# Fifteen instead of fourteen pairs of gate tiles by seven products, with three differences of h released from the pinned order

## The chip, the cores and the metric

The kernel runs on one core of a Trainium2 chip. The metric is the device time of one execution in microseconds (us), lower is better. TensorE (PE) multiplies, VectorE (DVE) and ScalarE (ACT) work elementwise, GpSimd (POOL) does some elementwise work and issues DMAs that add into their target, SyncE (SP) issues the other DMAs. Each engine takes its instructions in the order in which they stand in its own list, and waits on semaphores for the others.

## The reference, cut to what matters

Two groups of tokens go through one layer: 128 context tokens and 512 tokens of a grid, 640 together. Of the layer only the middle matters here:

```
h = rmsnorm(x, norm1_g) * (1 + sc1) + sh1            # 1024 features, 640 tokens
proj = h @ w_in                                      # input of four mixers a, b, c, d
y_a = gated short convolution; y_b = HGRN2 (a scan); y_c = neighbourhood attention; y_d = gMLP
g_a, g_b, g_c, g_d = split(sigmoid(h @ w_gate + b_gate), 4)
merged = g_a * (y_a @ w_br_a) + g_b * (y_b @ w_br_b) + g_c * (y_c @ w_br_c) + g_d * (y_d @ w_br_d)
x = x + g1 * (merged @ w_o)                          # then norm2 and the ConvFFN
```

`w_gate` is 1024 by 4096, each `w_br` 256 by 1024. A gate tile is 128 of the 1024 output features of one mixer, for all 640 tokens.

## The kernel before, in words

Features lie on the 128 partitions, tokens along a row. Every float32 operand is split into a high and a low part of type float32r, and every product is three matmuls (high by high, high by low, low by high), each 128x128 by 320 tokens. The high part is a copy by ScalarE, the low part a difference by VectorE.

**Plain gate tile** (`gate_tile`, line 997): 8 slices of features of h, and 2 of the mixer's y, in two halves of the tokens, three matmuls each: (8 + 2) x 2 x 3 = 60 matmuls by `gemm` (line 375 is the matmul). Its low part is made with a DMA by POOL (`low_dma`).

**Pair by seven products** (`g_pair`, line 1236): tiles n and n+4 of a mixer are computed together. Features are cut into two halves and tokens into two halves, so weights and h are 2 by 2 blocks, and seven products of sums of blocks (the scheme of Strassen and Winograd) replace eight. Each product is 12 matmuls over h (`gprod`, line 1186) and 3 over y (`bprod`, line 1195): 7 x 15 = 105 for the pair. In each pair the products over h stand in the order 1, 2, 6, 5, 7, 4, 3, with those over y between them. The sums of weight blocks for pair n+1 are made by VectorE while TensorE works on pair n (`g_s01`, `g_s23`, `g_b`, `g_c`, `g_zh`). `PAIRS` (line 990) lists them; `NPL` (line 46) says how many of the four pairs of the first mixer, d, are left to plain tiles. With `NPL = 2` four tiles of d (0, 1, 4, 5) are plain, and 14 pairs follow.

**Operands of the pairs** (`g_operands`, line 1038, a generator that is stepped beside the tiles): the products 7, 5 and 6 need sums of blocks of h. The float32 h waits in device memory (`hdr`, four blocks by feature half and token half). Three blocks are loaded: `d[:, 0]` and `d[:, 1]` (tile D) and `g` (tile G). Line 1051 makes three differences in place: a22 = a21 - a22, a21 = a11 - a21, a11 = a22 - a11, each 128x1280 on VectorE. `g_split` (lines 1077 and 1078) splits them into the tiles F (product 7), X1 (product 5) and X0 (product 6); F is free after the attention's last scores (`"scores"`), X1 and X0 after its last output (`"yc"`). Then the fourth block is loaded over a22 (line 1064), `y_load` (line 1080) puts y_d into D with a load by SP and an accumulating load by POOL, line 1071 adds a22 and a11, and `y_sums` (line 1089) makes four differences of y in D, from which `y_split` fills tile C.

**Order.** A helper keeps a clock of TensorE work and steps the side jobs (attention, convolution, operands) at due times on it, so program text is emitted interleaved. A scheduler of the framework may then move an instruction within its engine's list, unless `tc.keep_in_program_order` pins it. The differences of line 1051 are pinned; the whole pair part is pinned too (`fixed`, `ovec`, `oact`). `g_all` (line 1339) first drains the side jobs until the operands are emitted.

**Around the change** TensorE runs the attention's steps (scores at lines 842 and 845, transposes at 862, outputs at 879) between the last tiles of w_in and the first plain gate tiles. VectorE adds the bias and takes the maximum (849, 851), scales the exponentials (858, 859) and copies transposes back (2272).

Of the kernel before, what the change touches and what calls it, by code (L numbers as in the profile page):

```python
# [13 lines left out]
ALU = mybir.AluOpType  # L14
# [28 lines left out]
""".split()  # L43
WARM = 100
UE = [5, 3, 1]
NPL = 2
LOWD = ("ac", "ax", "ab", "d")
T = 640
TS = 512
# [21 lines left out]
def tile_step(ctx: ExitStack, tc: tile.TileContext, a: dict, outs: list, dbg=None):  # L71
# [58 lines left out]
    def region(tag, shape, dt=F32):  # L130
        return big.tile(shape, dt, tag=tag, name=nm(tag))
# [23 lines left out]
    ten, vec, pool = [Ordered(e, boot) for e in (nc.tensor, nc.vector, nc.gpsimd)]  # L155
# [236 lines left out]
    R = {}  # L392
# [524 lines left out]
    def in_tile(sec, n, w):  # L917
        ps = pg()
        gemm(ps, w, 0, 8, xhk, xlk)
        evac_in(sec, n, ps)  # L920
        if n == 1:
            R[sec + "_done"] = True
        if n == 1 and sec in starts:
            start(starts[sec](), 1.5, SLACK[sec])
            if sec == "cv":
                start(g_operands())
        if (sec, n) == AE[0]:
            start(ada_cols(range(16, AE[3]), "S0", col_home, HD[4], 10), AE[1])
# [60 lines left out]
    GI = dict(a=0, b=1, c=2, d=3)  # L989
    PAIRS = [(0, n) for n in range(NPL, 4)] + [(bi, n) for bi in range(1, 4) for n in range(4)]  # L990
    GPAIR = len(PAIRS)
# [46 lines left out]
    def g_operands():  # L1038
        while "cg" not in R:
            yield 1  # L1040
        d, g = region("D", [P, 2, 4, HC]), region("G", [P, 4, HC])
        yield 8
        for x, h, c in ((d[:, 0], 0, 1), (d[:, 1], 1, 1), (g, 0, 0)):
            yield 10
            nc.sync.dma_start(x, hdr[h, c])
        while "ya" not in R:
            yield 1
        yield 5
        a21, a22, a11 = d[:, 0], d[:, 1], g
        for o, x, y in ((a22, a21, a22), (a21, a11, a21), (a11, a22, a11)):  # L1050
            tc.keep_in_program_order(vec.tensor_tensor(o, x, y, ALU.subtract))
            yield 2
        gx["x"] = {}
        for i, h, c in ((1, 0, 0), (2, 1, 0), (4, 1, 1), (3, 0, 1)):
            cs = slice(c * HC, (c + 1) * HC)
            gx["x"][i] = xh[:, 4 * h:4 * h + 4, cs], xl[h][:, :, cs]
        for i, x, t, key in ((7, a21, "F", "scores"), (5, a22, "X1", "yc"), (6, a11, "X0", "yc")):
            while key not in R:
                yield 1
            y = region(t, [P, 2, 4, HC], F32R)  # L1060
            gx["x"][i] = y[:, 0], y[:, 1]
            g_split(i, x)
            if i == 5:
                nc.sync.dma_start(a22, hdr[1, 0])
            yield 1.5
        gx["t3"] = a22, a11
        gx["Y"] = a21.rearrange("p a t -> p (a t)")
        gx["S"] = a22.rearrange("p a t -> p (a t)").rearrange("p (i k c) -> p i k c", i=2, k=5)
        y_load(0)
        yield 7  # L1070
        vec.tensor_tensor(a22, a22, a11, ALU.add)
        y_sums()
        R["gx3"] = True

    def g_split(i, x):
        h, l = gx["x"][i]
        act(h, x, AF.Copy)
        vec.tensor_tensor(l, x, h.bitcast(F32), ALU.subtract)

    def y_load(bi):  # L1080

        if bi < 2:
            h, l = [R["y" + BR[bi]][:, i].rearrange("p k t -> p (k t)").bitcast(F32) for i in range(2)]
        else:
            h, l = [(ybd if bi == 2 else ycd)[:, i].rearrange("p k t -> p (k t)") for i in range(2)]
        nc.sync.dma_start(gx["Y"], h)
        opool.dma_start(gx["Y"], l, accum_op=ALU.add)

    def y_sums():

        a11, a21, a12, a22 = [gx["Y"][:, i * HC:(i + 1) * HC] for i in range(4)]
        for o, x, y, f in ((a22, a21, a22, ALU.subtract), (a21, a11, a21, ALU.subtract),
                           (a11, a22, a11, ALU.subtract), (a12, a12, a11, ALU.add)):
            ovec.tensor_tensor(o, x, y, f)
# [18 lines left out]
    def gp_id(p_):  # L1113
        return PAIRS[p_]
# [65 lines left out]
    def gprod(o, p_, i, first):  # L1180
        u, n = GPROD[i]
        w = gw[p_, u]
        xh_, xl_ = gx["x"][i]
        for k in range(4):
            for j, (h, x) in enumerate(((0, xh_), (0, xl_), (1, xh_))):
                mm(o, w[:, h, n, k, :], x[:, k, :], start=(first and k == 0 and j == 0),  # L1186
                   stop=(k == 3 and j == 2), skip_group_check=True)
            tick(0.44)
# [47 lines left out]
    def g_pair(p_, r):  # L1236
# [7 lines left out]
        bi, n0 = gp_id(p_)  # L1244
        new = n0 == (NPL if bi == 0 else 0)
        if new:
            gx["bi"] = bi
        if n0 == (NPL if bi == 0 else 0) + 1 and bi < 3:
            y_load(bi + 1)
# [68 lines left out]
        gprod(b2, p_, 3, False)  # L1318
        if n0 == (NPL if bi == 0 else 0) + 1 and bi < 3:
            y_sums()  # L1320
# [1131 lines left out]
    ten, vec, pool, act, mm = nc.tensor, nc.vector, nc.gpsimd, nc.scalar.activation, nc.tensor.matmul  # L2452
# [111 lines left out]
```

## Time and profile before

| what | value |
|---|---|
| median of 3 runs | 1001.57 us (1000.87 to 1004.2) |
| the profiled execution's own time | 1001.64 us |
| its span, first to last instruction | 999.9 us |
| TensorE busy | 987.3 us, 99% |
| VectorE busy | 860.6 us, 86% |
| ScalarE busy | 585.3 us, 59% |
| mean granted TensorE clock | 0.998 |

The page names a group of instructions by line, engine and tiles (`X<-D` writes X from D). The chain of waits is followed back from the last instruction; where it reads `PE` for a stretch, nothing but TensorE's own work decides there. A row of the timeline gives start, duration, engine, line, operation, tiles and in brackets the idle time before it with what ended it. A row of DMA issues gives the KB of one and the time from issue to landing.

### The profile page before, as it was taken

Reading aid. Unit: us, or ns where it says so; the run is one execution under the profiler, and the core shown is the slowest. Engines: PE = TensorE matmul, PEld = TensorE weight load, DVE = VectorE, ACT = ScalarE, POOL = GpSimd, SP = SyncE. Lnnn points to the kernel's source line nnn. Section 1 sums busy time; section 2 is a strip of 40 time slices with the busy share of each in tenths; the row PEclk is TensorE's granted clock in tenths of the full one; section 3 lists DMA queues with packets and bytes.
Section 4 is the critical chain, followed back from the end, with each engine's and each line's share of the span. In section 5 each row is a group of like instructions: output and inputs, shape, how many; then the busy total and the mean of one; then the engine's idle time right before and its main releaser. Section 6 shows DMA issues by size and latency. Waiting matters only on the chain.

```text
span 999.9 us, 18964 instructions
## 1 busy us (share of the span) xinstructions
PE 987.3 (99%) x7467; PEld 935.7 (94%) x7467; DVE 860.6 (86%) x1411; ACT 585.3 (59%) x1009; POOL 169.9 (17%) x227
## 2 busy tenths in 40 slices
PE   8999999999999999999999999999999999999997
PEld 6899999999999999999998799999999999888886
DVE  6678899878677989898879978999999998999796
ACT  6642343445555565555655376777777777756672
POOL 1000020323110223233010021222222222100004
PEclk9999999999999999999999999999999999999999
DMA  9874343498475999999348785766666666976842
GB/s 357 331 252 155 123 143 119 132 251 255 107 212 188 309 235 237 291 257 293 106 163 319 296 316 161 216 161 173 177 168 163 177 171 192 365 257 226 283 127 105
DMA packets 71016, 214.16 MB, mean 214 GB/s; under 512 B 9744, under 2 KB 24880, under 8 KB 68240
## 3 DMA queue, kind: packets, MB, share of 16 engines
q1 hardware_dynamic: 43968, 151.22, 43.2%
q0 software_dynamic: 26960, 61.75, 26.8%
q8 instruction: 58, 0.95, 0.4%
q14 instruction: 30, 0.25, 0.1%
HBM read 168.62 MB, written 48.51 MB: 217 GB/s over the span
## 4 chain that ended last, share of the span: by engine, by line
PE 89%; DVE 5%; DMA 3%; issue 2%; POOL 1%; SPq 0%; ACT 0%; POOLq 0%; DVEq 0%; ACTq 0%
PE g L1622 21%; PE m L1186 17%; PE g L375 16%; PE m L2094 9%; PE m L1622 5%; PE g L2094 4%; PE g L1195 3%; PE g L948 2%; PE m L1392 1%; PE m L1195 1%; PE m L539 1%; PE m L1617 1%; DMA S<-in_w_ada_dram 1%; DMA B<-in_w_ada_dram 1%; PE g L151 1%
## 5 line engine op out<-in xcount | busy, mean ns | idle before, releaser
L375 PE MATMUL g<-XH,w 128*128 128x320 f32 x704 | 169.4, 316 | 0.0
L375 PEld LDWEIGHTS g<-XH,w 128*128 128x128 f32 x704 | 120.3, 188 | 2.5 <-issue 1.2
L375 PE MATMUL g<-XL,w 128*128 128x320 f32 x352 | 108.7, 309 | 0.0
L1186 PE MATMUL m<-XH,w 128*128 128x320 f32 x336 | 79.8, 309 | 0.0
L375 PEld LDWEIGHTS g<-XL,w 128*128 128x128 f32 x352 | 66.3, 188 | 0.0
L2094 PE MATMUL m<-w,XH 128*128 128x512 f32 x246 | 58.5, 390 | 0.0
L1186 PEld LDWEIGHTS m<-XH,w 128*128 128x128 f32 x336 | 57.6, 188 | 0.0
L2094 PEld LDWEIGHTS m<-w,XH 128*128 128x128 f32 x246 | 46.1, 188 | 9.5
L1186 PE MATMUL m<-XL,w 128*128 128x320 f32 x168 | 51.9, 309 | 0.0
L151 ACT ACTIVATE w<-raw 128x640 fp32r<-128x640 f32 (+3 forms) x53 | 49.6, 952 | 3.2 <-PE g L375 2.0
L151 DVE TENSOR_TENSOR w<-raw,w 128x640 fp32r<-128x640 f32 (+3 forms) x43 | 43.9, 1039 | 1.9 <-ACT w L151 1.9
L151 POOL DMA_DIRECT2D wsum<-in_w_dn_dram x36 | 37.4, 1256 | 44.6 <-issue 40.6
L1186 PE MATMUL m<-X,w 128*128 128x320 f32 x264 | 42.6, 309 | 0.0
L1186 PEld LDWEIGHTS m<-X,w 128*128 128x128 f32 x264 | 39.7, 188 | 0.0
L151 DVE SCALAR_TENSOR_TENSOR X<-MG,p2t,X 128x641 f32<-128x641 f32 x44 | 38.9, 883 | 0.9 <-ACT X L151 0.2
L151 DVE SCALAR_TENSOR_TENSOR X<-X,p2t,X 128x641 f32<-128x641 f32 x44 | 38.9, 884 | 0.9
L1622 PE MATMUL g<-XL,w 128*128 128x320 f32 x240 | 38.6, 310 | 0.0
L1622 PE MATMUL g<-XL,C 128*128 128x320 f32 x240 | 38.3, 309 | 0.0
L151 ACT ACTIVATE gb<-m 128x320 f32<-128x320 f32 x28 | 12.3, 438 | 43.0 <-PE m L1186 43.0
L1622 PEld LDWEIGHTS g<-XL,w 128*128 128x128 f32 x240 | 36.0, 188 | 0.6 <-ACT MG L151 0.3
L1622 PEld LDWEIGHTS g<-XL,C 128*128 128x128 f32 x240 | 36.0, 188 | 0.0
L1186 PEld LDWEIGHTS m<-XL,w 128*128 128x128 f32 x168 | 31.5, 188 | 0.0
(612 smaller groups left out, 2852.0 us busy)
## 6 DMA issues: line engine op xcount, KB each, us to landing
wsum<-in_w_dn_dram POOLq DMA_DIRECT2D x30, 512.0 KB, 11.0
raw<-in_w_up_dram SPq DMA_DIRECT2D x30, 512.0 KB, 5.1
raw<-in_w_gp_dram SPq DMA_DIRECT2D x21, 640.0 KB, 6.0
raw<-in_w_in_dram SPq DMA_DIRECT2D x19, 512.0 KB, 4.3
H<-in_w_adt_dram SPq DMA_DIRECT2D x19, 512.0 KB, 4.1
raw<-wsum SPq DMA_DIRECT2D x12, 512.0 KB, 5.9
actx<-X POOLq DMA_DIRECT2D x22, 256.0 KB, 4.7
wsum<-wsum POOLq DMA_DIRECT2D x10, 512.0 KB, 10.3
```

Source lines behind the costliest of these rows:

```text
L151: r = f(*args, **kw)
L375: mm(o, w[:, h, k0 + k, :], r(k)[:, s], start=(k == 0 and i == 0), stop=(k == kt - 1 and i == 2))
L539: mm(m[W * g:W * g + W, (i - s0) * W:(i - s0 + 1) * W], lhs, rhs, start=True, stop=True, tile_position=(64 * par, W * g))
L948: mm(o, x(kx)[:, ts], w[:, h, k, :], start=(kx == 0 and i == 0), stop=(kx == 7 and i == 2))
L1186: mm(o, w[:, h, n, k, :], x[:, k, :], start=(first and k == 0 and j == 0), stop=(k == 3 and j == 2), skip_group_check=True)
L1195: mm(o, w[:, h, n, 4, :], x[l], start=(first and j == 0), stop=(j == 2), skip_group_check=True)
L1392: mm(m, mh[MHN[q]][:, hx, k % 2, t * P:(t + 1) * P], wo[q][:, hw, k % 2, :], start=(k == 0 and i == 0), stop=(k == 7 and i == 2))
L1617: mm(o, w[:, k, :], x[:, k, :], start=(first and not part and k == 0 and j == 0), stop=(part == 1 and k == 3), skip_group_check=True)
L1622: z = mm(o, w[:, k, :], x[:, k, :], start=(first and k == 0 and j == 0), stop=(k == 3 and j == 2), skip_group_check=True)
L2094: mm(ps, s[t // 4][:, hx, k, o:o + P], w[:, hw, k, c0:c1], start=first, stop=i == 2 and bi == len(batch) - 1 and k == len(ks) - 1, skip_gr ...
```

## The change

Two edits. `NPL` goes from 2 to 1: tiles 1 and 5 of mixer d are no longer two plain tiles but a fifteenth pair, which stands first. And in `g_operands` the three differences are emitted when the attention's last scores are out, instead of when y_a is ready and five units of the helper's clock later; they are no longer pinned, so the scheduler may place them.

```
-NPL = 2
+NPL = 1
...
         for x, h, c in ((d[:, 0], 0, 1), (d[:, 1], 1, 1), (g, 0, 0)):
             yield 10
             nc.sync.dma_start(x, hdr[h, c])
-        while "ya" not in R:
+        while "scores" not in R:
             yield 1
-        yield 5
         a21, a22, a11 = d[:, 0], d[:, 1], g
         for o, x, y in ((a22, a21, a22), (a21, a11, a21), (a11, a22, a11)):
-            tc.keep_in_program_order(vec.tensor_tensor(o, x, y, ALU.subtract))
+            vec.tensor_tensor(o, x, y, ALU.subtract)
             yield 2
```

Since a line goes, every later line of the kernel has a number lower by one: the differences are line 1050 after the change.

The first place is on VectorE, early in the attention, where the exponentials of its first two units (tile X_252) are scaled for the transposes of line 862 into m_3041. Before, it stands so:

```order
L858 RECIPROCAL ast_2877<-ast_2877 128x1 x2
L859 TENSOR_SCALAR X_252_2814<-X_252_2814,ast_2877 128x384 x2
L858 RECIPROCAL ast_2877<-ast_2877 128x1 x2
L859 TENSOR_SCALAR X_253_2815<-X_253_2815,ast_2877 128x384 x2
L2272 COPY MG_256_2818<-m_3041 128x384
L849 TENSOR_TENSOR X_252_2814<-m_3054,B_2816 128x384
L849 TENSOR_TENSOR X_252_2814<-m_3056,B_2816 128x384
L851 TENSOR_REDUCE ast_2877<-X_252_2814 128x1 x2
```

After the change, at the same place:

```order
L858 RECIPROCAL ast_2877<-ast_2877 128x1 x2
L1050 TENSOR_TENSOR D_2872<-D_2872 128x1280
L859 TENSOR_SCALAR X_252_2814<-X_252_2814,ast_2877 128x384 x2
L858 RECIPROCAL ast_2877<-ast_2877 128x1 x2
L1050 TENSOR_TENSOR D_2872<-G_2873,D_2872 128x1280
L2271 COPY MG_256_2818<-m_3041 128x384
L849 TENSOR_TENSOR X_252_2814<-m_3054,B_2816 128x384
L849 TENSOR_TENSOR X_252_2814<-m_3056,B_2816 128x384
L851 TENSOR_REDUCE ast_2877<-X_252_2814 128x1 x2
```

The first difference, which needs both loads of D, has moved ahead of the first scaling, and the second ahead of the first copy; the third stands 11 rows further on, ahead of the next copy.

The second place is on VectorE behind the last outputs of the attention (line 886, tile C), where the operands of the first pair are made. Before, it stands so, with four plain gate tiles still to go on TensorE:

```order
L1051 TENSOR_TENSOR D_2872<-D_2872 128x1280
L1051 TENSOR_TENSOR D_2872<-G_2873,D_2872 128x1280
L1078 TENSOR_TENSOR X_343_3649<-D_2872,X_343_3649 128x1280
L886 TENSOR_TENSOR C_2817<-m_3598,C_2817 128x8x16
L1051 TENSOR_TENSOR G_2873<-D_2872,G_2873 128x1280
L1014 TENSOR_TENSOR MG_337_3586<-g_3587,gt_3584 128x640
L1078 TENSOR_TENSOR F_3634<-D_2872,F_3634 128x1280
L1078 TENSOR_TENSOR X_344_3665<-G_2873,X_344_3665 128x1280
L1071 TENSOR_TENSOR D_2872<-D_2872,G_2873 128x1280
```

After, with two plain tiles to go (the w and G rows are weight sums of the first pair, the D<-D rows of 320 the differences of y, X_343 is the tile of product 5, X_345 that of product 6):

```order
L151 TENSOR_TENSOR D_2872<-D_2872 128x320 x2
L1077 TENSOR_TENSOR X_343_3623<-D_2872,X_343_3623 128x1280
L886 TENSOR_TENSOR C_2817<-m_3563,C_2817 128x8x16
L151 TENSOR_TENSOR D_2872<-D_2872 128x320 x2
L886 TENSOR_TENSOR C_2817<-m_3612,C_2817 128x8x16
L1014 TENSOR_TENSOR MG_340_3601<-g_3602,gt_3599 128x640
L1070 TENSOR_TENSOR D_2872<-D_2872,G_2873 128x1280
L1077 TENSOR_TENSOR X_345_3641<-G_2873,X_345_3641 128x1280
L151 TENSOR_TENSOR G_3507<-raw_3247,raw_3248 128x640
L151 TENSOR_TENSOR G_3507<-G_3507,raw_3248 128x640
L151 TENSOR_TENSOR raw_3248<-raw_3248 128x640
L151 TENSOR_TENSOR raw_3247<-G_3507,raw_3247 128x640
```

Behind these follow the split into XL (product 3) and the low part `w_3512<-G_3507` of the weight sums that products 5 and 6 take. The split into F now stands earlier, amid the last scores; the differences of y stand ahead of the split into X1, and only one plain tile's merge (line 1014) is left ahead of the weight sums where two were.

On SP the loads that feed this place before, with the writing out of y_c (`ycd`) and the fourth block ahead of y_d:

```order
L1122 DMA raw_3508<-in_w_gp_dram 128x1280
L905 DMA ycd<-C_2817 128x2560
L1064 DMA D_2872<-hdr 128x1280
L1086 DMA D_2872<-E_2765 128x1280
L1122 DMA raw_3849<-in_w_gp_dram 128x1280
```

And after:

```order
L1121 DMA raw_3707<-in_w_gp_dram 128x1280
L1085 DMA D_2872<-E_2765 128x1280
L1063 DMA D_2872<-hdr 128x1280
L905 DMA ycd<-C_2817 128x2560
L1121 DMA G_3708<-in_w_gp_dram 128x1280
```

The load of y_d (`D<-E`) has moved ahead of the fourth block, and right behind a weight load of the second pair.

More of the change, by code (lines that the diff above doesn't have):

```diff
@@ L45 @@
 UE = [5, 3, 1]
-NPL = 2
+NPL = 1
 LOWD = ("ac", "ax", "ab", "d")
@@ L1045, in g_operands @@
             nc.sync.dma_start(x, hdr[h, c])
-        while "ya" not in R:
+        while "scores" not in R:
             yield 1
-        yield 5
         a21, a22, a11 = d[:, 0], d[:, 1], g
         for o, x, y in ((a22, a21, a22), (a21, a11, a21), (a11, a22, a11)):
-            tc.keep_in_program_order(vec.tensor_tensor(o, x, y, ALU.subtract))
+            vec.tensor_tensor(o, x, y, ALU.subtract)
             yield 2
```

## The prediction

> **What bounds the kernel now.** I read the page, then the chain of waits over the stretch that the change touches, then the timeline of VectorE and of the DMA queues there.
>
> ```profile
> PE 987.3 (99%) x7467; PEld 935.7 (94%) x7467; DVE 860.6 (86%) x1411; ACT 585.3 (59%) x1009; POOL 169.9 (17%) x227
> ```
>
> TensorE has no free time to speak of, so matmuls that go away are saved whole and any wait of TensorE is lost whole. The chain of waits, from the attention to the first pair (start, us, what):
>
> ```profile
> 224.44 4.59 PE g L375 x30
> 229.04 0.66 PE m L862 x6
> ...
> 282.38 27.04 PE g L375 x183
> 309.41 1.76 PE m L1186 x12
> 311.17 0.44 PE g L1195 x3
> 311.61 3.52 PE m L1186 x24
> ...
> 319.09 0.44 PE g L1195 x3
> ```
>
> It is TensorE without a break. The 183 matmuls at 282.38 are the last 3 of one plain gate tile and three whole ones; the first pair starts at 309.41. Product 6 of the pair follows the first 27 matmuls, at 309.41 + 1.76 + 0.44 + 1.76 = 313.37, and the row of 319.09 is that product's part over y, the first user of tile C.
>
> VectorE is the helper with least to spare (us, then busy time by engine):
>
> ```profile
> 229.00:234.00 5.00, 5.00 (x39) 4.67 (x38) 3.80 (x6) 3.20 (x7) 2.36 (x3) 1.00 1.05 404
> 234.00:239.00 5.00, 5.00 (x43) 4.49 (x42) 4.96 (x14) 2.55 (x4) 0.26 (x1) 1.00 0.78 197
> 239.00:244.00 5.00, 5.00 (x44) 4.75 (x42) 4.52 (x13) 1.80 (x5) 2.08 (x3) 1.00 0.87 197
> ```
>
> In these 15 us VectorE works 13.28, and idles 1.72.
>
> **Part 1: fewer matmuls.** Two plain tiles are 120 matmuls, at 27.04 / 183 = 0.148 us each 17.7 us. The new pair is 105 matmuls at 3.52 / 24 = 0.147 us, 15.4 us. The gain is 2.3 us, certain as long as TensorE is fed. The weights loaded are the same bytes, and the low parts that POOL's adding DMAs made for the two tiles are now VectorE's. Nothing else in the change can save time, so 2.3 us, or 0.23%, is the most that it can win; about 0.3%, 3.0 us, is what a measurement of this kernel can tell from no change.
>
> **Part 2: the first difference, in its new place.** The order puts it on VectorE ahead of the scaling of the attention's first exponentials, and it needs both loads of tile D. The rows: VectorE at that place, the pinned difference where it ran before, and the second load of D with its time to landing.
>
> ```profile
> 227.06 0.21 DVE L858 RECIPROCAL ast<-ast 128x1 f32<-128x1 f32 x2
> 227.25 0.75 DVE L859 TENSOR_SCALAR X<-X,ast 128x384 f32<-128x384 f32 x2
> ...
> 277.11 1.48 DVE L1051 TENSOR_TENSOR D<-D 128x1280 f32<-128x1280 f32 x1
> ```
>
> ```profile
> 221.71 1.26 SPq L1045 DMA_DIRECT2D D<-hdr  x1
> ```
>
> ```profile
> D<-hdr SPq DMA_DIRECT2D x1, 640.0 KB, 9.7
> ```
>
> Up to here both programs have the same order on every engine, so the load lands as before, at 221.71 + 9.7 = 231.4. VectorE gets to the difference at 227.27 and can only wait. The difference ends at 231.4 + 1.48 = 232.9, the scaling 0.75 later at 233.6. TensorE stands at the transposes of line 862, which read what was scaled, from 229.04: it waits 4.6 us. Its order has no other matmul in between, so that is lost.
>
> Behind it stand the other two differences, 2 x 1.48, within the next 10 us. Followed row by row with the durations before, VectorE ends the next two scalings at 240.65, where TensorE would want them at 240.5, and the copy behind the third difference at 243.0, which frees the bank that the scores of 242.4 need. That adds some 0.6 us (bounds 0 and 1.2: none if VectorE's 1.72 us of idle time take it, 1.2 if the copies of the next step are late too). Part 2 costs 5.2 us, between 4.6 and 5.8.
>
> **Part 3: two plain tiles less between the attention and the first pair.** TensorE now has 63 matmuls behind the attention instead of 183, 9.3 us: the first pair starts at 282.38 + 9.3 + 5.2 = 296.9, and wants product 6 at 300.85 and tile C 319.09 - 309.41 = 9.7 us behind its start, at 306.6. Here is the chain that must be through by then, by rows of before.
>
> POOL's last adding DMA of a plain tile frees a weight buffer, and SP's next load waits for it; `D<-E` (y_d) now follows that load.
>
> ```profile
> 263.57 0.89 POOL L151 DMA_DIRECT2D w<-raw  x1 [3.43 <-ACT w L151]
> ...
> 268.75 0.33 SPq L1122 DMA_DIRECT2D raw<-in_w_gp_dram  x1
> ```
>
> These follow TensorE's progress, so they come 5.2 us later, at 273.95, and `D<-E` goes out at 274.3; the split into F that it must wait for, now amid the last scores, ends by 273.1. How long such loads take, alone or beside others:
>
> ```profile
> w<-raw POOLq DMA_DIRECT2D x1, 640.0 KB, 5.1
> D<-A SPq DMA_DIRECT2D x1, 640.0 KB, 3.4
> D<-hdr SPq DMA_DIRECT2D x1, 640.0 KB, 6.5
> D<-E SPq DMA_DIRECT2D x1, 640.0 KB, 9.0
> raw<-in_w_gp_dram SPq DMA_DIRECT2D x1, 640.0 KB, 5.0
> raw<-in_w_gp_dram SPq DMA_DIRECT2D x1, 640.0 KB, 4.0
> D<-E POOLq DMA_DIRECT2D x1, 640.0 KB, 7.9
> ycd<-C SPq DMA_DIRECT2D x1, 1280.0 KB, 5.4
> G<-in_w_gp_dram SPq DMA_DIRECT2D x1, 640.0 KB, 5.0
> ```
>
> `D<-E` took 9.0 beside three other transfers before, 3.4 is the same form for y_a; now only the 640 KB ahead of it run with it, which makes 1280 KB, and I take the row of that size, 5.4: landed 279.7. POOL's adding load went out 0.6 us behind the landing before (286.59 + 9.0 = 295.6, and 296.18 in the rows below), so 280.3; alone such a load takes 5.1, beside others 7.9, I take the middle, 6.5: landed 286.8.
>
> The first two differences of y wait for it at the head of VectorE, and queued behind them are the split into X1, the attention's last two outputs, the merge that frees a PSUM bank, and all sums of the first pair. VectorE's rows for these before, with the loads among them:
>
> ```profile
> 286.59 0.52 SPq L1086 DMA_DIRECT2D D<-E  x1
> ```
>
> ```profile
> 296.18 0.87 POOL L151 DMA_DIRECT2D D<-E  x1 [8.83 <-DMA D<-E]
> ```
>
> ```profile
> 294.57 0.82 DVE L151 TENSOR_TENSOR G<-raw,raw 128x640 f32<-128x640 f32 x1
> ...
> 296.90 0.82 DVE L151 TENSOR_TENSOR raw<-G,raw 128x640 f32<-128x640 f32 x1
> 304.07 2.07 DVE L151 TENSOR_TENSOR D<-D 128x320 f32<-128x320 f32 x4 [6.35 <-DMA D<-E]
> 306.05 0.82 DVE L1014 TENSOR_TENSOR MG<-g,gt 128x640 f32<-128x640 f32 x1
> 306.79 1.48 DVE L151 TENSOR_TENSOR w<-G,w 128x1280 fp32r<-128x1280 f32 x1
> 308.19 1.49 DVE L1078 TENSOR_TENSOR XL<-D,XH 128x1280 fp32r<-128x1280 f32 x1
> ...
> 313.97 0.82 DVE L151 TENSOR_TENSOR D<-raw,G 128x640 f32<-128x640 f32 x1
> 314.83 0.83 DVE L151 TENSOR_TENSOR D<-D,G 128x640 f32<-128x640 f32 x1
> 315.57 1.22 DVE L151 TENSOR_TENSOR C<-D,C 128x640 fp32r<-128x640 f32 x2
> ```
>
> Two of the four differences of y (half of 2.07) and the split into X1 (1.4 from start to start, as the rows of 306.79 and 308.19) take 2.4: 289.2. Only then may the fourth block of h be loaded over a22; 5.0, as a load beside POOL's took (bounds 4.0 and 6.5): 294.2. The sum of line 1071, now 1070, takes 1.49 (a row of that size above), the split into X0 1.4, four weight sums 3.15 (294.57 to 297.72), the split into XL 1.4, the low part of the weight sums 1.49: 303.1. That is 2.25 us behind product 6. From there the load into G (its buffer is now free) takes 5.0 and three rows of VectorE 2.4 (313.97 to the first C): 7.5 in all, 310.6, against 306.6 + 2.25. So TensorE waits 4.0 us in the first pair, in two pieces of about 2.25 and 1.75.
>
> With all loads at their short ends (3.4, 5.1, 4.0) the chain is 4.4 us earlier and nothing waits; with the long ones (9.0, 7.9, 6.5) it is 6.5 later, and 10.5 are lost.
>
> **Sum.** -2.3 + 5.2 + 4.0 = +6.9 us. Against the profiled execution's own 1001.64 that is 1008.5; the median of the runs, 1001.57, is 0.07 from it, so no correction is made.
>
> **The rivals.** Early wait alone: the loads of part 3 are at their short ends and the pair's operands come in time. Then -2.3 + 4.9 = +2.6, 1004.2. For it: `D<-E` no longer meets `ycd`. Against it: four DMAs follow one another through it, and all must be quick.
>
> Not slower: the loads of h themselves are quick. If the second half of D lands by 227.3, 5.6 us behind its issue instead of 9.7, VectorE doesn't wait; the difference alone makes TensorE wait 229.45 - 229.04 = 0.4, and with the same quick queue nothing in part 3: -2.3 + 0.4 = -1.9, 999.7. For it: 640 KB have landed in 3.4 to 5.1 elsewhere. Against it: the transfers share of 1.05 in the window from 229 (last but one column) is a full queue, and nothing ahead of it changes.
>
> The clock: a wait of 4.6 us is longer than any that TensorE has before. If the matmuls behind it were granted a lower clock, and the 24 of a row of 3.52 took twice as long, that is 3.5 more: 1012.0. The rows speak against it: with no matmul at all over 3 us at the end, the clock column stays at 1.00.
>
> ```profile
> 993.00:996.00 3.00, 0.00 (x0) 0.00 (x0) 1.93 (x7) 0.72 (x1) 0.55 (x1) 1.00 0.44 175
> ```
>
> [...]
>
> **How the numbers follow.** The forecast, both waits: 0.62. Early wait alone: 0.17. Lower clock on top: 0.10. Not slower: 0.05. Longer loads than taken, 1013 and above: 0.06. The likeliest gives 1008.5. From the early wait alone (with part 2 at its low end, -2.3 + 4.6 = 2.3, 1003.9) to 1013.0 the range leaves out the not-slower case, the longest loads and some of the clock: 1003.8 to 1013.0. Faster by over 0.3% is beyond the 2.3 us that can be won: 0.02. Within 0.3%: the not-slower case and half of the early wait alone, 0.13. Slower: 0.85.
>
> **What would show it.** Right: VectorE idle for about 4 us ahead of line 1050's first row, released by the DMA into D, and TensorE idle 4.6 us ahead of line 862 near 229; a pair from 296.9 on that takes 19 us instead of 15.4, idle ahead of products 6 and of its first part over y in C, while all later pairs take 15.4; 15 pairs. Wrong: no wait at line 862 (then part 2 falls and the sum is near 1003); the first pair at 15.4 (part 3 falls); later pairs longer, or a clock under 1.00 behind the wait.

## The result, and the profile after

The changed kernel takes 1011.1 us in the median of 6 runs (1009.43 to 1013.84), the kernel before, run beside it, 1001.93 (1000.87 to 1004.2). The ratio is 1.0093, with a 95% interval of 1.0073 to 1.0113: slower by 0.9%. The profiled execution took 1009.65 us, its span is 1007.9, 8.0 more than before.

The engines' totals say little, as before: TensorE is busy in 98% of the span. The list of TensorE's waits (us in total, times, the longest) says where the time went:

```profile
PE m L862 <- DVE X L859: 4.3, 1, 4.3
PE g L1194 <- ACT gt L1003: 2.8, 1, 2.8
...
PE m L1391 <- DVE w L324: 1.3, 1, 1.3
```

The first two are new; the last was 0.6 before. The timeline of VectorE at the first wait, and of TensorE:

```profile
231.03 1.49 DVE L1050 TENSOR_TENSOR D<-D 128x1280 f32<-128x1280 f32 x1 [4.09 <-DMA D<-hdr]
232.44 0.74 DVE L859 TENSOR_SCALAR X<-X,ast 128x384 f32<-128x384 f32 x2
...
240.77 1.47 DVE L1050 TENSOR_TENSOR G<-D,G 128x1280 f32<-128x1280 f32 x1
242.16 0.55 DVE L2271 COPY MG<-m 128x384 f32<-128x384 f32 x1
```

```profile
228.39 0.31 PE L375 MATMUL g<-XH,w 128*128 128x320 f32 x1
233.00 0.89 PE L862 MATMUL m<-cst,X 128*128 128x128 f32 x6 [4.29 <-DVE X L859]
```

VectorE stands 4.09 us at the first difference until the second load of D is there; the scaling queued behind it is done 0.7 us after the difference, and only then can TensorE transpose. The granted clock (third column from the end) in stretches of 1 us, behind the first wait and around the end of the second:

```profile
233.00:234.00 1.00, 1.00 (x8) 0.77 (x10) 1.00 (x4) 0.08 (x1) 0.00 (x0) 0.84 1.09 367
234.00:235.00 1.00, 1.00 (x6) 0.83 (x8) 1.00 (x2) 0.41 (x1) 0.00 (x0) 0.50 1.07 225
...
301.00:302.00 1.00, 0.00 (x0) 0.00 (x0) 1.00 (x2) 1.00 (x3) 0.00 (x0) 0.97 0.00 0
...
305.00:306.00 1.00, 1.00 (x7) 1.00 (x7) 1.00 (x2) 1.00 (x3) 0.00 (x0) 0.82 0.98 297
```

From 233.68 on (0.84 is 0.32 us at half) and again from 301.94 on, the clock reads 0.50 for some 3.4 us. From the moment that its matmuls go on, TensorE reads as fully busy there: the loss shows only in the clock column and in longer matmuls (the three over y at 302.43, below, take 1.17 us; the three of the same line at 318.36, in the second pair at a clock of 1.00, take 0.60). The chain of waits, before the change and after it, from the same transposes to the second step's matmuls:

```profile
229.04 0.66 PE m L862 x6
...
238.56 4.16 PE g L375 x27
```

```profile
233.00 0.89 PE m L862 x6
...
244.14 4.16 PE g L375 x27
```

Before, 9.52 us lie between the two; after, 11.14. So the stretch costs 4.0 us by the wait (TensorE stands 4.29 us, but it came there 0.3 earlier than before) and 1.6 behind it, 5.6 in all.

The first pair starts at 297.67 and stops one product after its start. TensorE's rows, the last one of the first product over h and the next, which is that product's part over y:

```profile
299.29 0.31 PE L1185 MATMUL m<-XH,w 128*128 128x320 f32 x1
302.43 1.17 PE L1194 MATMUL g<-E,w 128*128 128x320 f32 x3 [2.83 <-ACT gt L1003]
```

`g` is a PSUM bank that TensorE's matmuls write (`g<-E,w`) and that the second plain tile still holds until ScalarE has taken its sigmoid from it (`gt<-g`). ScalarE at that place:

```profile
299.80 1.27 ACT L151 ACTIVATE w<-G 128x1280 fp32r<-128x1280 f32 x1 [1.79 <-DVE G L151]
300.97 0.72 ACT L151 ACTIVATE S<-raw 128x640 fp32r<-128x640 f32 x1
301.60 0.77 ACT L1003 ACTIVATE gt<-g,cst 128x640 f32<-128x640 f32 x1
```

The sigmoid (last row) needs nothing but its bank, which was complete at 296.1; it stands behind the high parts of the first pair's weight sums and of Z (the row `S<-raw`, the weights of product 7), and these wait for VectorE. VectorE in turn waits for the chain of loads into D:

```profile
287.63 1.02 DVE L151 TENSOR_TENSOR D<-D 128x320 f32<-128x320 f32 x2 [5.34 <-DMA D<-E]
...
295.15 1.49 DVE L1070 TENSOR_TENSOR D<-D,G 128x1280 f32<-128x1280 f32 x1 [3.04 <-DMA D<-hdr]
296.56 1.48 DVE L1077 TENSOR_TENSOR X<-G,X 128x1280 fp32r<-128x1280 f32 x1
298.08 0.82 DVE L151 TENSOR_TENSOR G<-raw,raw 128x640 f32<-128x640 f32 x1
...
302.55 1.48 DVE L151 TENSOR_TENSOR w<-G,w 128x1280 fp32r<-128x1280 f32 x1
```

The second pair, which is the first of before, starts at 316.60. The first matmuls of the first and of the second pair, before the change and after it:

```profile
309.25 0.31 PE L1186 MATMUL m<-XH,w 128*128 128x320 f32 x1
...
323.77 0.31 PE L1186 MATMUL m<-XH,B 128*128 128x320 f32 x1
```

```profile
297.67 0.31 PE L1185 MATMUL m<-XH,w 128*128 128x320 f32 x1
...
316.60 0.31 PE L1185 MATMUL m<-XH,B 128*128 128x320 f32 x1
```

From its start to the next pair's, the first pair took 14.5 us before and takes 18.9 now. It is 14.5 and not the 15.4 of a whole pair because the last 6 of its 105 matmuls stand behind the next pair's first product. So the first pair loses 4.4 us: 3.0 by the wait, with the usual distance between two matmuls taken off, and 1.4 behind it at half clock.

### The profile page after: what moved, and what is told of

Its sections match the earlier page's. It is cut to its first block, busy times and chain, and to the rows that moved or that the text cites. A ratio compares the mean times of both kernels' runs of the same rounds, so it can differ in the third digit from the quotient of the medians.

```text
span 1007.9 us, 18957 instructions
## 1 busy us (share of the span) xinstructions
PE 988.0 (98%) x7452; PEld 935.7 (93%) x7452; DVE 869.3 (86%) x1424; ACT 587.5 (58%) x1017; POOL 168.1 (17%) x225
## 4 chain that ended last, share of the span: by engine, by line
PE 86%; DMA 6%; DVE 4%; issue 2%; POOL 1%; ACT 0%; SPq 0%; POOLq 0%; DVEq 0%; ACTq 0%
PE g L1621 21%; PE m L1185 18%; PE g L375 10%; PE m L2093 9%; PE m L1621 5%; PE g L2093 4%; PE g L1194 3%; PE g L948 2%; PE m L1391 2%; PE m L151 2%; DMA D<-hdr 1%; PE g L151 1%; PE m L1194 1%; DMA D<-E 1%; PE m L539 1%
## 5 line engine op out<-in xcount | busy, mean ns | idle before, releaser
L375 PE MATMUL g<-XH,w 128*128 128x320 f32 x640 | 155.6, 318 | 0.0
L375 PEld LDWEIGHTS g<-XH,w 128*128 128x128 f32 x640 | 110.2, 189 | 2.6 <-issue 1.4
L375 PE MATMUL g<-XL,w 128*128 128x320 f32 x320 | 99.1, 310 | 0.0
L1185 PE MATMUL m<-XH,w 128*128 128x320 f32 x368 | 88.1, 311 | 0.0
L1185 PEld LDWEIGHTS m<-XH,w 128*128 128x128 f32 x368 | 63.9, 190 | 0.0
L375 PEld LDWEIGHTS g<-XL,w 128*128 128x128 f32 x320 | 60.6, 189 | 0.0
L1185 PE MATMUL m<-XL,w 128*128 128x320 f32 x184 | 57.2, 311 | 0.0
L151 DVE TENSOR_TENSOR w<-raw,w 128x640 fp32r<-128x640 f32 (+3 forms) x46 | 47.1, 1040 | 2.4 <-ACT w L151 2.4
L1621 PE MATMUL g<-XL,w 128*128 128x320 f32 x240 | 38.6, 310 | 0.0
L1621 PEld LDWEIGHTS g<-XL,w 128*128 128x128 f32 x240 | 36.0, 188 | 0.6 <-ACT MG L151 0.3
L1185 PEld LDWEIGHTS m<-XL,w 128*128 128x128 f32 x184 | 35.0, 190 | 0.0
```

Of the source, the lines that this page charges most:

```text
L151: r = f(*args, **kw)
L375: mm(o, w[:, h, k0 + k, :], r(k)[:, s], start=(k == 0 and i == 0), stop=(k == kt - 1 and i == 2))
L1621: z = mm(o, w[:, k, :], x[:, k, :], start=(first and k == 0 and j == 0), stop=(k == 3 and j == 2), skip_group_check=True)
```

## The experiments

Ratios are to the kernel before, run beside each kernel, with 95% intervals.

**1. The first edit alone** (`NPL = 1`, differences pinned as before).

> First edit alone: one plain tile less per half, the differences pinned where they were. Theory (two separate losses, the early wait of 4.3 us with 1.7 us of slow clock behind it belongs to the moved differences): no wait at the transposes near 229, clock 1.00 there, the first pair starts near 292; its operands are still late, as the differences now stand behind the attention, so some 2 to 5 us of wait in the first pair: 1002 to 1005. Rival (the differences' place costs nothing of its own, the missing cover of the two plain tiles is all): 1008 to 1011, with the whole loss in the first pair.

1007.37 us, ratio 1.0059 (1.0047 to 1.0072). TensorE's waits in that stretch:

```profile
PE g L1195 <- DVE C L151: 2.2, 1, 2.2
PE m L1186 <- DVE w L151: 0.7, 1, 0.7
```

No wait at the transposes and a clock of 1.00 there, so the early wait belongs to the second edit. The first pair is late by itself, but at other rows: it waits for the operands (the low part of w and the tile C), since here the sigmoid stands ahead of the splits. Another 0.7 us are put down to ScalarE's `w`, and the clock falls behind the 2.2. From its start to the next pair's the first pair takes 22.2 us here, 7.7 too many. The time lies between what the theory and the rival gave, and the whole loss is in the first pair, as the rival had it; it takes experiments 3 and 7 to tell the two.

**2. The second edit alone** (`NPL = 2`, differences as in the change).

> Second edit alone: two plain tiles per half as before, the differences in free order. Theory: wait of 4.3 us at the transposes near 229 and clock at half for some 3.4 us behind it (1.7 us), nothing in the first pair: 1001.6 + 6.0 = 1007.6, between 1006 and 1009. Rival (the clock falls only where both edits meet): 1001.6 + 4.3 = 1005.9. Rival (a wait so early is taken up later): 1001 to 1003.

1020.27 us, ratio 1.0183 (1.0169 to 1.0196): all three expectations fall. The early wait is there as foretold; beside it the list of waits has a second one, and ScalarE's rows name it:

```profile
PE g L375 <- ACT gt L1003: 8.7, 1, 8.7
PE m L862 <- DVE X L859: 4.3, 1, 4.3
```

```profile
305.34 0.74 ACT L151 ACTIVATE S<-raw 128x640 fp32r<-128x640 f32 x1 [12.87 <-DVE raw L151]
305.99 0.78 ACT L1003 ACTIVATE gt<-g,cst 128x640 f32<-128x640 f32 x1
```

It is the same place in ScalarE's queue, at a larger price: the high part of Z stands ahead of a plain tile's sigmoid and waits 12.87 us for VectorE's sums. The chain of waits leads back from there to a weight load, which now stands on SP behind the fourth block of h: it went out at 292.59, when an adding load by POOL had landed after 9.8 us, and took 10.2 itself. So the two edits don't add up: 5.6, 18.5 and together 9.2 us.

**3. The differences held back.** They read a one that is written behind the reciprocal of unit 4's softmax sum (`HOLD = 4`), so they stay in free order, but stand behind the loads.

```
             vec.reciprocal(st[:, 2:3], st[:, 1:2])
+            if u == HOLD:
+                R["hold"] = const.tile([P, 1], F32, name="hold")
+                vec.tensor_scalar(R["hold"], st[:, 2:3], 0.0, 1.0, ALU.mult, ALU.add)
...
-            vec.tensor_tensor(o, x, y, ALU.subtract)
+            vec.scalar_tensor_tensor(o, x, R["hold"][:, 0:1], y, ALU.mult, ALU.subtract)
```

> Both edits, but the differences read a one that is written behind the softmax sums of the third step, so that they stay in free order and stand behind the load instead of ahead of it. Theory: the early wait and its slow clock go (4.3 + 1.7 us), the first pair's wait of 2.8 us and the slow clock behind it stay: about 6 us under the changed kernel, 1003 to 1005. Rival (the 4.3 us only move to the first pair, since the chain of loads into D doesn't get earlier): 1007 to 1010 with a longer wait in the first pair.

1005.77 us in the median, 1003.17 in the profiled execution, ratio 1.0037 (1.0024 to 1.005). Nothing waits at the transposes; the pair's wait (lines are numbered four higher here) and the clock at its end and behind it:

```profile
296.50 0.70 PE L1198 MATMUL g<-E,w 128*128 128x320 f32 x3 [2.78 <-ACT gt L1007]
```

```profile
295.00:300.00 5.00, 3.50 (x24) 3.50 (x25) 5.00 (x6) 5.00 (x9) 0.00 (x0) 1.00 0.18 43
```

The early loss is separate from the first pair's, as the theory has it; the chain moves with TensorE. The profiled execution lies in the theory's range, the median 0.8 us above it. What I had not foretold: behind a wait of the same length the clock stayed at 1.00 in this execution. Its mean clock is 0.999; the other four runs have 0.994 to 0.997 and take 2.3 to 3.1 us longer; that the clock fell in them is argued from these means, not shown.

**4. The same, with the first pair's weight sums in tile B** instead of G, which holds a block of h until the sum of line 1070 has read it.

```
-        s = gw[p_, "S"] = gx["S"] if p_ else region("G", [P, 2, 5, P])
+        s = gw[p_, "S"] = gx["S"] if p_ else region("B", [P, 2, 5, P])
```

> As the run before, and the weight sums of the first pair go to tile B, which is free by then, instead of tile G, which they can only have when the last sum of h has read it. Theory (the first pair waits for ScalarE, whose sigmoid stands behind the split of these sums, and they wait for G): the wait of 2.8 us and its slow clock go, 1.0 to 1.5 us at most are left: 999.3 to 1001.5. Rival (the loads into D set the first pair's start whatever is queued behind them): as the run before, 1003 to 1005.

1001.0 us, ratio 0.9996 (0.9987 to 1.0005). The pair's wait is gone; one row of 0.58 is left, for the first plain tile's merge, which now stands behind the sums on VectorE:

```profile
291.00 1.99 PE L376 MATMUL g<-E,w 128*128 128x320 f32 x12 [0.58 <-DVE MG L1018]
```

**5. The sigmoid ahead.** The changed kernel, with the last plain tile's sigmoid pinned ahead of the first pair's splits, and its merge with it; the order of all other instructions is the same.

> The changed kernel, with the last plain tile's sigmoid and its merge put ahead of the splits of the first pair's weight sums on ScalarE and VectorE; no other instruction moves. Theory A (the chain of loads into D, sums and splits is late whatever is queued beside it): the 2.8 us wait for the sigmoid goes, and TensorE waits 2.4 to 3.1 us at product 6 for the low part of the sums instead, so the time stays within 1.5 us of the changed kernel's 1009.7 to 1011. Theory B (the queue on ScalarE alone is the loss): the wait and its slow clock go, 4 us less, 1005.5 to 1007.

1012.29 us, ratio 1.0107 (1.0092 to 1.0122). TensorE's rows:

```profile
304.68 0.56 PE L1188 MATMUL m<-X,w 128*128 128x320 f32 x2 [2.46 <-ACT ga L151]
305.82 3.03 PE L1188 MATMUL m<-X,w 128*128 128x320 f32 x10 [0.58 <-DVE w L151]
```

Theory A: the wait moves to product 6 (3.04 us in two pieces, once for ScalarE, once for the low part of the sums), where the prediction had it. ScalarE's queue decides where TensorE stops. That it stops is decided by the chain of loads, through tile G: with the sums in tile B (experiment 7) they run from 291.24, ahead of the fourth block, which lands at 294.5 there and at 295.1 in the changed kernel, and the wait is gone.

**6. The wait filled.** The changed kernel, with 64 matmuls that nobody reads ahead of the transposes.

```
+            if u == 0:
+                for _ in range(64):
+                    mm(m[:, 384:512], xh[:, 0, 0:P], xh[:, 0, 0:P], start=True, stop=True)
```

> The changed kernel, with 64 matmuls of 128x128 that nobody reads between the 9 matmuls of the tile before and the transposes that wait near 229 (into columns of the transposes' bank that are not used). They take some 3.9 us of the 4.3 that TensorE stands idle there. Theory (the wait itself costs 4.3, and 1.7 more because the clock falls in it): the clock stays at 1.00 behind the transposes, the stretch up to 243 is 1.5 us shorter. Rival (the low clock has nothing to do with the idle time): clock 0.50 as before, no time won.

1013.89 us, ratio 1.0127 (1.0112 to 1.0142). They took 0.11 us each, not the 0.06 that I had scaled from the columns, so they overran the wait by 2.7. But the clock stayed up:

```profile
228.63 7.26 PE L863 MATMUL m<-XH 128*128 128x128 f32 x64
235.72 0.84 PE L865 MATMUL m<-cst,X 128*128 128x128 f32 x6
```

```profile
235.00:240.00 5.00, 5.00 (x40) 4.67 (x40) 4.88 (x9) 1.40 (x4) 1.43 (x2) 1.00 0.45 88
```

```profile
245.14 0.42 PE L375 MATMUL g<-XH,w 128*128 128x320 f32 x1
```

From the transposes at 235.72 to the second step's first matmul at 245.14 it is 9.4 us. The same two rows lie 9.6 us apart in the kernel before (228.88 to 238.49) and 11.1 in the changed kernel (233.00 to 244.07), so the price of the clock is 1.5 to 1.65 us. Nothing of it shows in the time: the matmuls themselves take 2.7 more, and in the first pair TensorE then waits 4.6 us.

**7. The sums in B alone**, the differences as in the change.

> The changed kernel, with the first pair's weight sums in tile B instead of tile G, so that they need not wait for the last sum of h; the differences stay where the change puts them. Theory (two separate losses): the wait near 302 and the slow clock behind it go, the one near 229 stays: 4.3 us under the changed kernel's profiled 1009.7, 1005 to 1007. Rival (the early wait delays the chain so that the first pair waits anyway): 1008 and above.

1007.63 us, ratio 1.006 (1.0045 to 1.0075); 1006.49 in the profiled execution:

```profile
PE m L862 <- DVE X L859: 4.4, 1, 4.4
PE g L375 <- DVE MG L1014: 0.8, 1, 0.8
```

As the theory has it: each of the two losses can be taken away without the other. The profiled execution lies in the range foretold, the median 0.6 us above it.

**8. The second edit alone, with Z's high part on VectorE.** One row of ScalarE's order goes, one of VectorE's comes.

```
-        oact(gx["Z"][:, 0, 0], r[1][:, 1], AF.Copy)
+        if p_:
+            oact(gx["Z"][:, 0, 0], r[1][:, 1], AF.Copy)
+        else:
+            vec.tensor_copy(gx["Z"][:, 0, 0], r[1][:, 1])
```

> The second edit alone, with one row moved: the high part of Z of the first pair is made by VectorE instead of ScalarE, where it stands ahead of a plain tile's sigmoid and waits for a weight load. Theory (this one row in ScalarE's queue makes the 8.7 us wait): the sigmoid comes 12 us earlier, what is left is 1.5 to 2.5 us for the merge on VectorE behind the same sums: 1012 to 1014.5. Rival (TensorE waits for the loads themselves): 1018 to 1021.

1011.95 us, ratio 1.0106 (1.0089 to 1.0123), 8.3 under experiment 2:

```profile
PE g L375 <- DVE MG L1014: 2.6, 1, 2.6
```

So it was that one row: the 8.7 us become 2.6, for the merge that stands behind the same sums on VectorE.

**9. The wait filled with 37 matmuls.**

> As the run with 64 idle matmuls, with 37: at the 0.11 us each that those took they end by 232.7, before the transposes can start. Theory: the transposes start at 233.0 as in the changed kernel, the clock behind them stays at 1.00, and the second step's 27 matmuls start 1.65 us earlier than the changed kernel's 244.14, at 242.5; what the first pair's wait does with it is not foretold. Rival: clock 0.50 behind them and 244.1.

1014.06 us, ratio 1.0124 (1.0111 to 1.0137). TensorE's rows, and the clock:

```profile
228.71 4.24 PE L863 MATMUL m<-XH 128*128 128x128 f32 x37
...
244.01 0.48 PE L842 MATMUL m<-F 64*128 64x256 f32 x1 [1.42 <-DVE MG L2274]
```

```profile
234.00:235.00 1.00, 1.00 (x11) 0.74 (x9) 1.00 (x2) 0.49 (x1) 0.00 (x0) 1.00 1.05 228
```

The transposes start at 233.23 and the clock stays at 1.00, and yet the second step's matmuls start at 244.9, not at 242.5: TensorE, now faster, stops 1.42 us for the second step's copy, which is late because VectorE has had no pause since the load of D landed. VectorE's order isn't quite the change's, though: here, as in experiment 6, all three differences stand ahead of the first copy. So that in the changed kernel the slow clock covers a part of that lateness is likely, but not shown. In the first pair this run waits 4.8 us, 2.0 more than the changed kernel. Its fourth block of h took 6.97 us to land where the changed kernel's took 5.05, which makes up nearly all of that; why it did stays open.

**10. Experiment 4 with the merge ahead of the sums.**

> As the run with the held differences and the sums in B, with the sums emitted behind the plain tiles, so that the first plain tile's merge stands ahead of them on VectorE. Theory: the 0.6 us wait for that merge goes and no other comes: 0.6 us less than that run, 1000.4 in the median, 0.13% under the kernel before. Rival: product 6 waits again for the low part of the sums, 1 to 2 us: 1002 to 1003.

1001.78 us, ratio 1.0007 (0.9997 to 1.0018). The wait for the merge goes, and one of 0.82 us for the sigmoid comes back: inconclusive. No version was measurably faster than the kernel before; at most 2.3 us could be won.

## Why the prediction was right, and where it was not

**Part 1** holds as far as it can be seen. In experiment 4, with both waits out, the first matmul behind the pairs starts at 523.42, against 524.43 in the kernel before: 1.0 us won. Some 0.7 more went to the new wait at the merge and 0.8 to short delays in the attention, and 0.3 of the gain was there ahead of the attention's transposes. That leaves 2.2, near the 2.3.

**Part 2** said 5.2 us, between 4.6 and 5.8; 5.6 were measured. The mechanism is shown by experiments 1, 3 and 7: the load ended VectorE's wait at 231.03, for a forecast of 231.4. The parts differ: 4.0 instead of 4.6 for the wait, and 1.6 behind it, where I had put 0.6 for late copies. It was the clock; so that the sum came out in its range is in part luck.

**The clock** was the step that I misjudged. I gave it 0.10 and took the row from 993, 3 us without a matmul at 1.00, for evidence against it. The next 3 us of the same kernel, the one before, read:

```profile
996.00:999.00 3.00, 0.00 (x0) 0.00 (x0) 0.00 (x0) 0.00 (x0) 0.00 (x0) 0.53 0.44 175
```

The clock falls there some 3.4 us after the last matmul (that one ends at 992.8, and 0.53 over 3 us puts the fall at 996.2). In the changed kernel it reads 0.50 for 3.4 us from 233.68 on. Half of that is the 1.7 us of the expectations, an estimate; the same rows with and without the fall (experiment 6) put its price at 1.5 to 1.65 us. The rival's 3.5 us on top were too much for one fall, but there were two, 1.6 and 1.4 us, and the second stood in no rival. Whether the clock simply comes on top stays open: in experiment 9, without it, 1.4 us come back as a wait for a late copy, in an order of VectorE unlike the change's.

**Part 3** got the chain nearly row by row, from the load's issue (274.3 forecast, 275.20 in the trace) through its durations:

```profile
D<-E SPq DMA_DIRECT2D x1, 640.0 KB, 5.5
D<-E POOLq DMA_DIRECT2D x1, 640.0 KB, 6.3
D<-hdr SPq DMA_DIRECT2D x1, 640.0 KB, 5.0
```

to the end of the low part of the weight sums (303.1 forecast, 304.03 in the trace). That all three came within 0.2 us of the 5.4, 6.5 and 5.0 chosen is in part luck: each was picked between bounds that lay 2.5 to 5.6 apart, and in experiment 9 the last of the three takes 6.97. The loss is 4.4 us (18.9 - 14.5) for a forecast of 4.0; the 19 us that I gave for the pair were counted over all of its 105 matmuls, so that 18.9 meets them is chance. The step that failed is "TensorE waits 4.0 us in the first pair, in two pieces of about 2.25 and 1.75", at product 6 and at tile C. TensorE stopped earlier, 3.0 us at the first product over y, then lost 1.4 to the clock, and came to product 6 and to tile C late enough to wait for neither. I had followed VectorE's queue and the DMAs, and not ScalarE's, where the same sums stand ahead of the sigmoid that frees a PSUM bank. Experiment 2 shows what one row ahead of a sigmoid in ScalarE's queue does: its bank was complete at 296.35, and it ran at 305.99, behind a row that had waited 12.87 us. Experiment 5 shows that the forecast wait was real and stood right behind: with the sigmoid out of the way, product 6 waits 3.04.

**The sum.** At the first matmul behind the pairs (line 1391, before the change 1392) the changed kernel stands at 532.66 and the kernel before at 524.43, so the change costs 8.2 us there; 6.9 were forecast. It is -2.3 for the matmuls, 5.6 in the attention's first step, 0.5 in small delays of the attention behind it (one step takes 6.9 us where the others take 6.5), and 4.4 in the first pair. Behind the pairs little is added: the wait at line 1391 grew from 0.6 to 1.3 (0.8 to 1.9 in the experiments, with 14 pairs as with 15; its cause is open), and two waits of 0.5 together at line 1436 are gone. The median of 1011.1 is 1.5 above the profiled execution. The other runs of the changed kernel have mean clocks of 0.991 to 0.996 beside its 0.995, and the slowest two have the lowest; that they met more stretches at half clock is argued from these means, not shown.

## What to carry to other kernels

An instruction that is set free goes where the scheduler believes its data to be ready; before that is trusted, look up in the trace when its load really lands, and what is queued behind it on that engine. When operands come late, follow the queue of every engine that frees a bank or a buffer for the waiting one, not only of the engine that makes the operands. Price a wait of TensorE with the slow clock that may stand behind it (here 1.4 us for a wait of 2.83 and 1.6 for one of 4.29), and expect part of what is saved in one place to come back as the next wait.

## What the runs showed of the hardware

The clock fell in or behind each of the eight waits of TensorE of 4.3 to 8.7 us (in the changed kernel and experiments 2 and 5 to 9), and in or behind shorter ones too: 2.83 us (the changed kernel), 2.46 and 0.58 us (experiment 5), 2.21 us (experiment 1) and 1.95 us (experiment 5, at line 1396). It did not fall behind those of 2.78 us (experiment 3's profiled execution) and 2.57 us (experiment 8). Two rows for the shortest, of experiments 1 and 5:

```profile
307.00:308.00 1.00, 0.22 (x1) 0.22 (x2) 1.00 (x2) 0.00 (x0) 0.00 (x0) 0.93 0.62 254
```

```profile
568.00:569.00 1.00, 1.00 (x3) 0.85 (x4) 1.00 (x3) 0.53 (x1) 0.00 (x0) 0.60 0.61 57
```

So the length of a wait alone doesn't decide; what does beside it was not shown. Nor does the fall come at one place of a wait: in the changed kernel it came at 233.68, 0.68 us after the wait of 4.29 had ended, and at 301.94, when TensorE had stood for 2.35 of the 2.83 us. Both times the clock then read 0.50 for 3.4 us. It can be longer: worked out from rows of 5 us, and estimated with 0.50 throughout, the clock was low for 6.8 us in experiment 8 (0.64 and 0.68 in the 10 us from 230) and for 10.2 in experiment 2 (0.74, 0.50 and 0.74 in the 15 us from 300). And two waits of one length differ: 2.83 us cost 1.4 more by the clock in the changed kernel, while behind 2.78 us in experiment 3's profiled execution it read 1.00.

The 64 matmuls of 128x128 in experiment 6 took 7.26 us, 0.11 each, where 24 of 128x320 take 3.52 in the kernel before, 0.147 each.
